# Remainders of projection weights kept in DRAM between the two halves of a sequence

## The chip, the cores and the metric

The kernel runs on one core of a Trainium2 chip. The metric is the device time of one execution in microseconds (us). Three runs of the kernel before took 1563.96, 1564.00 and 1564.34 us; the median is 1564.0 us.

The engines of the core are called here as the profile calls them: PE (TensorE, matrix products), DVE (VectorE), ACT (ScalarE), POOL (GpSimd) and SP (SyncE, which here only issues DMAs). Each engine runs its own instructions in order; a semaphore holds an instruction until what it needs has been done elsewhere, and everything behind it on that engine waits with it.

## What is computed

One layer of a decoder trunk, on 1024 rows of 1024 numbers in float32:

```
h = rms_norm(x, norm_mix)
proj = h @ w_in                        # 1024 x 8192
xa, ga, q, f, v, g, m_a, m_b = split(proj, 8 parts of 1024)
xa = causal_depthwise_conv(xa, conv_w, conv_b)
y_a = rg_lru(xa, w_r, b_r, w_i, b_i, lam) * gelu(ga)
o = rms_norm(hgrn2_chunkwise(silu(q), k(f), log_f(f), v), hg_norm)
y_b = o * silu(g)
y = sigmoid(m_a) * y_a + sigmoid(m_b) * y_b
x = x + y @ w_out
h = rms_norm(x, norm_mlp)
x = x + square(relu(h @ w_up)) @ w_down
out = rms_norm(x, norm_final)
```

`rg_lru` is a linear recurrence over the rows whose gates come from two block-diagonal products (`w_r`, `w_i`); `hgrn2_chunkwise` is gated linear attention with eight heads, done by blocks.

## The kernel before

**Products in two parts.** PE multiplies in a format with a shorter mantissa (`fp32r`). To keep float32's precision, each operand is split in a high part H, the value cast to `fp32r`, and a remainder L, the value less H. A product is then three matmuls, H by H, H by L and L by H (`mm3`, L131 to L136; in the profile the three lines are L134, L135 and L136). The split is made by `split` (L88 to L90): a cast on ACT (L89), then a subtraction on DVE (L90) that reads the raw value and the cast one.

**The mixer.** The first part of the program, up to about 520 us, makes the projections `xa`, `q`, `f`, `v` and the products of the recurrence's gates (`rg`), with the recurrence (`rg_lru`) and the attention (`hgrn`) beside them. The rows are in two chunks (`c`) of 512 and the heads in four pairs (`p`), so there are eight stages, chunk 0 with pairs 0 to 3 and then chunk 1 with pairs 0 to 3. Each pair has nine weight tiles of 128x1024 (512 KB): two each for `xa`, `q`, `f` and `v`, and one for `rg`. The list `pair_tiles` has the order of use; its 72 entries hold every one of the 36 tiles twice, once for each chunk, since the tiles aren't kept in between. The first half of the mixer is entries 0 to 35, the second half 36 to 71.

**Loading and splitting weights.** `load_w` takes one of four `raw` buffers and issues a load on SP's queue (L97). `split_w` takes two of six buffers (tag `w`) for H (`wH`) and L (`wL`) of the tile, and splits. `get_w` asks for a tile when PE's code comes to use it and has two more split ahead. A `raw` buffer is free when its cast and its subtraction are done; a `w` buffer is free when PE has done the last matmul that reads it. Which engine instruction comes where is set by a scheduler that simulates the program and takes priorities (`tc.high_priority`) and marks for program order (`tc.keep_in_program_order`) into account; PE's order in the mixer is pinned.

**Inside a stage.** `hgrn` of one pair runs while the next stage's projections run on PE: it is written as calls `go(n)` that let n steps of the next stage's generator pass, between blocks of its own products. The names that matter: `f`, `kk`, `q` are the gate, key and query tiles; `kc`, `qb`, `qf`, `seg` are products of them made on DVE (L508); `sc` are banks with the blocks' scores (L518, L637, L648); `pk` are the transposes of `kk` on PE (L674), copied by ACT to `kT` (L679); `pkv` are the key by value products (L684); `sn` are the states, and `po` the outputs. `kk` is scaled for the last time on DVE just before `pk`. The copy `kc` to `kk`, the convolution (`xc`, L413), the recurrence (`ri`, `rw`), and the subtractions for weight tiles share DVE with it. A stage begins with the `v` products of the pair before, which use the two `v` tiles together.

**SP's queue.** It holds, in one order, the loads of `raw`, of `x`, the stores of the recurrence's result (`hd`, L474), and the stores of sums and differences of the normed rows made on POOL for a later part (`cd`, L327).

Of the kernel before, what the change touches and what calls it, by code (L numbers as in the profile page):

```python
# [10 lines left out]
F32 = mybir.dt.float32  # L11
# [7 lines left out]
P = 128  # L19
# [27 lines left out]
def trunk(ctx: ExitStack, tc: tile.TileContext, x, wts, mlp, pv, gains, mask_f, mask_u, out):  # L47
    nc = tc.nc
    V, A, G, PE = nc.vector, nc.scalar, nc.gpsimd, nc.tensor
# [4 lines left out]
    dram = ctx.enter_context(tc.tile_pool(name="dram", bufs=1, space=DRAM))  # L54
# [12 lines left out]
    pair_tiles = []  # L67
    for i in range(NC * NPAIR):
        at = (0, 1, 2, 3, 4, 6, 5)
# [6 lines left out]
    for c in range(NC + 1):  # L76
        seq += [wts[MIX_TILES + j] for j in range(OUT_TILES)]
    most = [n_mix]
    ready, made = {}, [0]


    in_order = [True]
# [1 line left out]
    def keep(ins):  # L84
        if in_order[0]:
            tc.keep_in_program_order(ins)

    def split(src, h, lo):  # L88
        keep(A.copy(h, src))  # L89
        keep(V.tensor_tensor(out=lo, in0=src, in1=h.bitcast(F32), op=ALU.subtract))  # L90
# [9 lines left out]
    def split_w(i, raw):  # L100
        h = wp.tile([P, 1024], F32R, tag="w", name=f"wH{i}", bufs=6)
        lo = wp.tile([P, 1024], F32R, tag="w", name=f"wL{i}", bufs=6)
        with tc.high_priority(400):
            split(raw, h, lo)
        return h, lo

    raws = []

    def fill_w(n):
        while made[0] < min(n, most[0]):  # L110
            i = made[0]
            raw = raws.pop(0) if raws else load_w(i)
            ready[made[0]] = split_w(i, raw)
            made[0] += 1
# [650 lines left out]
    def stage(i):  # L765
        c, p = where(i)
        got = gots[i]
        if i == 0:
            yield from v_steps(c, p, got, lambda tt: None)
        elif i > 1:  # L770
            yield from v_of(i)

        def more(n):
            with tc.high_priority(400):
                transposed(xn1[n], hT[1], n, f"x1{n}")

        hooks = {at: lambda n=n: more(n) for at, n in {2: ((4, 1),), 3: ((2, 2), (6, 3))}.get(i, ())}
        px = yield from hooked(project_steps(c, f"xa{c}{p}"), hooks)
        xc, xps = conv_in(c, p, px)
        if i == 0:  # L780
            parameters()
            tc.keep_in_program_order(V.tensor_copy(mu, mu32.to_broadcast([P, 7, 8, 32])))
            pinned[0] = True
        yield
        if i == 1:
            gots[0]["tail"]()
            transposed(xn1[0], hT[1], 0, "x10")
        if i > 4:
            combos_on(2)

        def convolve():
            got["xc"] = conv(c, p, xc, xps, None)

        pq = yield from hooked(project_steps(c, f"q{c}{p}"), {} if i == 1 else {6: convolve})
        got["q1"] = q_of(c, p, pq)
        yield
        fs = hooked(project_steps(c, f"f{c}{p}"), {6: convolve} if i == 1 else {})
        for _ in range(5 if i != 1 else 7):
            next(fs)
            yield  # L800
        if i > 3:
            combos_on(1 if i == 4 else 2)
        if i == 1:
            pf = yield from fs
            got["f"], got["kk"] = f_of(c, p, pf)
            yield
        yield from rg_lru(c, p, got, *got["xc"])
        if i > 0:
            gots[i - 1]["normalised"]()
        for n in ((0,), (1,), (2, 3))[i] if i < 3 else ():  # L810
            xn1[n] = next_rows(n)
        if i != 1:
            pf = yield from fs
            got["f"], got["kk"] = f_of(c, p, pf)
# [14 lines left out]
    def last_stage():  # L829
        yield from v_of(NC * NPAIR)  # L830
        combos_on(2)
        w = [next_w(), next_w()]
        g2 = []
        for c in range(NC):
            pp = yield from plain(c, w, "g")
            g = mt(("xc", "h")[c], f"g2{c}", (P, 2, T))
            g2.append(g)
            for s in range(2):
                o = g[:, s if c == 0 else 1 - s, :]
                A.activation(o, pp[s], AF.Sigmoid)  # L840
                V.tensor_tensor(out=o, in0=o, in1=pp[s], op=ALU.mult)
            if c == 0:
                combos_on(1)
            yield
        w = [next_w(), next_w()]
        for c in range(NC):
            pp = yield from plain(c, w, "mb")
            g = g2[c]
            t = mt("ri", f"smb{c}", (P, 2, T))
            for s in range(2):  # L850
                A.activation(t[:, s if c == 0 else 1 - s, :], pp[s], AF.Sigmoid)
            V.tensor_tensor(out=g, in0=g, in1=t, op=ALU.mult)
            if c == 0:
                nc.scalar.dma_start(g2d[:, 0:2, :], g)
                gots[-1]["normalised"]()
                yield
        on_T(NC - 1, NPAIR - 1, gots[-1])
        nc.scalar.dma_start(g2d[:, 2:4, :], g2[1])
# [29 lines left out]
    for i in range(NC * NPAIR):  # L888
        rest = stage(i + 1) if i + 1 < NC * NPAIR else last_stage()
# [336 lines left out]
    rest = []  # L1226
# [320 lines left out]
```

## Time and profile before

| what | us |
|---|---|
| median of three runs | 1564.0 |
| the profiled execution | 1564.07 |
| its span, first to last instruction | 1562.2 |
| PE busy | 1523.0 |
| DVE busy | 1205.4 |
| ACT busy | 818.5 |
| POOL busy | 155.5 |

The span is the time from the first to the last instruction in the profile of one execution; the time of the same execution is 1.9 us longer. Busy times are sums over the span. PE's matmuls overlap, so a busy PE is not one at its peak. A row of a time line has its start, its length, engine and line, operation, tile written and tiles read, shape and count, and in brackets the idle time of the engine ahead of it with what ended it. Buffer numbers are left out of names in the profile, so `wL` there is any remainder tile of weights. Rows with SPq are issues of DMAs. A row of waits has who waited for whom, the sum in us, how often, and the longest. A row on a DMA issue has how often, the size, and the median time from issue to landing.

### The profile page before, as it was taken

Reading aid. Unit: us, or ns where it says so; the run is one execution under the profiler, and the core shown is the slowest. Engines: PE = TensorE matmul, PEld = TensorE weight load, DVE = VectorE, ACT = ScalarE, POOL = GpSimd, SP = SyncE. Lnnn points to the kernel's source line nnn. Section 1 sums busy time; section 2 is a strip of 40 time slices with the busy share of each in tenths; the row PEclk is TensorE's granted clock in tenths of the full one; section 3 lists DMA queues with packets and bytes.
Section 4 is the critical chain, followed back from the end, with each engine's and each line's share of the span. In section 5 each row is a group of like instructions: output and inputs, shape, how many; then the busy total and the mean of one; then the engine's idle time right before and its main releaser. Section 6 shows DMA issues by size and latency. Waiting matters only on the chain.

```text
span 1562.2 us, 23154 instructions
## 1 busy us (share of the span) xinstructions
PE 1523.0 (97%) x9072; PEld 1271.9 (81%) x9072; DVE 1205.4 (77%) x1706; ACT 818.5 (52%) x1341; POOL 155.5 (10%) x187
## 2 busy tenths in 40 slices
PE   7999999999999999999999989999999999999998
PEld 6878888888788887888888777888888878888886
DVE  5798596696786928786856589888888988888877
ACT  5657757557467435454533376777777631111113
POOL 1013110233624600000000000000000000000000
PEclk9999999999999999999999999999999999999999
DMA  6233233233442274432338862766666675666642
GB/s 235 97 105 109 68 109 108 79 122 120 141 136 95 95 289 181 137 135 81 135 108 308 283 216 99 298 252 250 245 243 242 226 286 225 252 253 253 252 192 108
DMA packets 75341, 280.07 MB, mean 179 GB/s; under 512 B 7776, under 2 KB 20192, under 8 KB 62304
## 3 DMA queue, kind: packets, MB, share of 16 engines
q1 hardware_dynamic: 72208, 267.58, 46.6%
q10 hardware_dynamic: 3024, 11.01, 1.9%
q8 instruction: 71, 1.16, 0.3%
q14 instruction: 38, 0.31, 0.1%
HBM read 193.63 MB, written 84.93 MB: 178 GB/s over the span
## 4 chain that ended last, share of the span: by engine, by line
PE 79%; DVE 11%; ACT 6%; issue 2%; DMA 2%; POOL 0%; DVEq 0%; SPq 0%; ACTq 0%; POOLq 0%
PE dX L134 4%; PE dX L135 4%; PE dX L136 4%; PE uX L134 3%; PE uX L135 3%; PE uX L136 3%; PE gX L134 3%; PE gX L135 3%; PE gX L136 3%; PE dY L135 2%; PE dY L136 2%; PE dY L134 2%; PE uY L134 2%; PE uY L135 2%; PE uY L136 2%
## 5 line engine op out<-in xcount | busy, mean ns | idle before, releaser
L90 DVE TENSOR_TENSOR wL<-raw,wH 128x1024 fp32r<-128x1024 f32 x100 | 123.9, 1240 | 76.2 <-ACT wH L89 75.8
L89 ACT CAST wH<-raw 128x1024 fp32r<-128x1024 f32 x100 | 104.9, 1049 | 78.7 <-PE po L135 26.2
L1456 DVE TENSOR_TENSOR acc<-acc,dX 128x512 f32<-128x512 f32 x128 | 85.1, 685 | 29.2 <-PE dX L136 28.9
L89 ACT CAST wA<-q 128x512 fp32r<-128x512 f32 x46 | 28.5, 621 | 139.1 <-PE dX L136 101.0
L1456 DVE TENSOR_TENSOR acc<-acc,dY 128x512 f32<-128x512 f32 x64 | 43.5, 686 | 15.7 <-PE dY L136 14.5
L136 PE MATMUL po<-wH,y 128*128 128x512 f32 x128 | 50.0, 391 | 0.0
L134 PE MATMUL po<-wH,y 128*128 128x512 f32 x128 | 50.0, 391 | 0.0
L135 PE MATMUL po<-wL,y 128*128 128x512 f32 x128 | 50.0, 391 | 0.0
L1321 ACT ACTIVATE b<-b 128x512 f32<-128x512 f32 x48 | 30.1, 630 | 29.5 <-DVE b L1320 29.4
L157 POOL TENSOR_TENSOR rstd_h<-rstd_h,mhalf 128x1 f32<-128x1 f32 x8 | 5.6, 700 | 379.0 <-DVE rstd_h L156 379.0
L90 DVE TENSOR_TENSOR wA<-q,wA 128x512 fp32r<-128x512 f32 x46 | 31.6, 687 | 13.6 <-ACT wA L89 13.6
L413 DVE SCALAR_TENSOR_TENSOR xc<-xp,pvt,xc 128x512 f32<-128x512 f32 x48 | 40.4, 862 | 0.0
L927 DVE TENSOR_TENSOR s<-q,q 128x512 f32<-128x512 f32 x46 | 31.6, 689 | 2.8 <-DMA q<-mlp_in 2.3
L326 POOL TENSOR_TENSOR stt<-r,stt 128x256 fp32r<-128x256 f32 x16 | 21.1, 1337 | 118.5 <-ACT stt L325 113.5
L932 DVE TENSOR_TENSOR s<-q 128x512 f32<-128x512 f32 x46 | 31.6, 688 | 0.3
L716 ACT ACTIVATE on<-po 128x128 f32<-128x128 f32 x64 | 16.9, 281 | 27.9 <-PE po L712 27.9
L1322 ACT ACTIVATE b<-b 128x512 f32<-128x512 f32 x48 | 30.0, 630 | 1.1
L136 PEld LDWEIGHTS po<-wH,y 128*128 128x128 f32 x128 | 24.1, 188 | 4.9
L135 PEld LDWEIGHTS po<-wL,y 128*128 128x128 f32 x128 | 24.0, 188 | 4.9
L134 PEld LDWEIGHTS po<-wH,y 128*128 128x128 f32 x128 | 24.0, 188 | 4.8
L615 ACT COPY kk<-kc 128x512 f32<-128x512 f32 x8 | 5.0, 622 | 43.1 <-DVE kc L508 43.1
L622 POOL TENSOR_SCALAR scT<-dd 32x256 f32<-32x256 f32 x32 | 21.5, 671 | 52.7 <-DVE dd L537 36.1
(2528 smaller groups left out, 5418.6 us busy)
## 6 DMA issues: line engine op xcount, KB each, us to landing
raw<-wts_in SPq DMA_DIRECT2D x96, 512.0 KB, 3.6
q<-mlp_in SPq DMA_DIRECT2D x92, 512.0 KB, 3.6
x<-x_in SPq DMA_DIRECT2D x8, 512.0 KB, 6.0
hd<-ri SPq DMA_DIRECT2D x16, 256.0 KB, 3.0
od<-onT ACTq DMA_DIRECT2D x8, 512.0 KB, 5.6
cdT<-stT SPq DMA_DIRECT2D x16, 256.0 KB, 3.6
o<-od SPq DMA_DIRECT2D x4, 1024.0 KB, 7.0
h<-hd SPq DMA_DIRECT2D x4, 1024.0 KB, 4.8
```

What stands on the lines that cost most here:

```text
L89: keep(A.copy(h, src))
L90: keep(V.tensor_tensor(out=lo, in0=src, in1=h.bitcast(F32), op=ALU.subtract))
L134: pin(PE.matmul(o, ah, bh, start=first, stop=False, **how))
L135: pin(PE.matmul(o, ah, bl, start=False, stop=False, **how))
L136: pin(PE.matmul(o, al, bh, start=False, stop=last, **how))
L413: ins = V.scalar_tensor_tensor(xc[:, s, :], xp[:, j : j + T], pvt[:, PV_CW + 8 * j + u : PV_CW + 8 * j + u + 1], xc[:, s, :], op0=ALU.mult ...
L622: G.tensor_scalar(scT[32 * b : 32 * b + 32, :, 32 * b : 32 * b + 32], dd[32 * b : 32 * b + 32, :, :], 1.0, 0.0, op0=ALU.mult, op1=ALU.add,)
L927: V.tensor_tensor(out=sa[:, 0, :], in0=a21, in1=a22, op=ALU.add)
L932: V.tensor_tensor(out=sb[:, 0, :], in0=a21, in1=a11, op=ALU.add)
L1321: A.activation(b[:, at, :], b[:, at, :], AF.Relu, scale=-1.0 if at == 2 else 1.0)
L1322: A.activation(b[:, at, :], b[:, at, :], AF.Square)
L1456: V.tensor_tensor(out=dst, in0=dst, in1=banks[bk, pr], op=op)
```

## The change

When a weight tile of the mixer is split for the first time, and the same tile comes again later in `pair_tiles`, its remainder is stored to a DRAM tile of its own. When it comes for the second time, only the cast is done; the remainder is loaded from DRAM into the L buffer. Both DMAs are issued on SP's queue. The numbers that the matmuls read are the same.

```
-    ready, made = {}, [0]
+    ready, made, rests = {}, [0], {}
...
     def split_w(i, raw):
         h = wp.tile([P, 1024], F32R, tag="w", name=f"wH{i}", bufs=6)
         lo = wp.tile([P, 1024], F32R, tag="w", name=f"wL{i}", bufs=6)
+        at = pair_tiles[i] if i < len(pair_tiles) else None
         with tc.high_priority(400):
+            if at in rests:
+                A.copy(h, raw)
+                nc.sync.dma_start(lo.bitcast(F32), rests[at])
+                return h, lo
             split(raw, h, lo)
+        if at is not None and at in pair_tiles[i + 1 :]:
+            rests[at] = dram.tile([P, 1024], F32, tag=f"rest{at}", name=f"rest{at}")
+            nc.sync.dma_start(rests[at], lo.bitcast(F32))
         return h, lo
```

In all, 36 subtractions leave DVE (100 of this form become 64), 36 stores join SP's queue in the first half, and 36 loads join it in the second half. A `raw` buffer of the second half is free when its cast is done. The lines of the kernel below the change move down by eight, so L508 becomes L516 and so on.

**DVE in the first stage of the second half that has the attention of chunk 1, pair 0.** The rows from the partial copies of scores (`dd`) to the last scaling of `kk`; the first number behind a name is its chunk and pair or its place in the list of tiles. Before:

```order
L537 COPY_PREDICATED dd10_3301<-mu_122,sc2_10_3611 128x32x2
L413 SCALAR_TENSOR_TENSOR xc11_3528<-xp13_3532,pvt_77,xc11_3528 128x512
L90 TENSOR_TENSOR wL50_3718<-raw50_3715,wH50_3717 128x1024
L537 COPY_PREDICATED dd10_3301<-mu_122,sc8_10_3644 128x8x24
L90 TENSOR_TENSOR xcL11_3742<-xc11_3528,xcH11_3741 128x1024
L537 COPY_PREDICATED dd10_3301<-mu_122,sc8_10_3644 128x8x16
L411 COPY xp14_4233<-xcar_124 128x3
L537 COPY_PREDICATED dd10_3301<-mu_122,sc8_10_3644 128x8x8
L487 SCALAR_TENSOR_TENSOR q111_3757<-sq11_3758,par_123,pj_q11_0_3591 128x256x2
L90 TENSOR_TENSOR wL51_3768<-raw51_3765,wH51_3767 128x1024
L487 SCALAR_TENSOR_TENSOR q111_3757<-sq11_3758,par_123,pj_q11_1_3592 128x256x2
L508 TENSOR_TENSOR kk10_3293<-kk10_3293,seg10_3303 128x8x64
```

DVE in the same place, now:

```order
L545 COPY_PREDICATED dd10_3373<-mu_122,sc2_10_3683 128x32x2
L90 TENSOR_TENSOR xcL11_3814<-xc11_3600,xcH11_3813 128x1024
L545 COPY_PREDICATED dd10_3373<-mu_122,sc8_10_3716 128x8x24
L419 COPY xp14_4305<-xcar_124 128x3
L545 COPY_PREDICATED dd10_3373<-mu_122,sc8_10_3716 128x8x16
L545 COPY_PREDICATED dd10_3373<-mu_122,sc8_10_3716 128x8x8
L495 SCALAR_TENSOR_TENSOR q111_3829<-sq11_3830,par_123,pj_q11_0_3663 128x256x2
L495 SCALAR_TENSOR_TENSOR q111_3829<-sq11_3830,par_123,pj_q11_1_3664 128x256x2
L516 TENSOR_TENSOR kk10_3365<-kk10_3365,seg10_3375 128x8x64
```

The subtractions of tiles 50 and 51 are gone, the last step of the convolution (`xc`) stands further up, and the rest is in nearly the same order.

**SP's queue in the second half, around the second `v` tile (tile 44) of the same stage.** `raw` with a number is the load of that tile. Before:

```order
L97 DMA raw46_3335<-wts_in 128x1024
L97 DMA raw47_3468<-wts_in 128x1024
L97 DMA raw48_3498<-wts_in 128x1024
L97 DMA raw49_3593<-wts_in 128x1024
L97 DMA raw50_3715<-wts_in 128x1024
L97 DMA raw51_3765<-wts_in 128x1024
```

SP's queue in the same place, now; `rest` with a number is the DRAM tile of that weight tile:

```order
L97 DMA raw46_3407<-wts_in 128x1024
L107 DMA wL43_3270<-rest7_157 128x1024
L97 DMA raw47_3540<-wts_in 128x1024
L107 DMA wL44_3291<-rest8_183 128x1024
L97 DMA raw48_3570<-wts_in 128x1024
L107 DMA wL45_3404<-rest9_600 128x1024
L97 DMA raw49_3665<-wts_in 128x1024
L107 DMA wL46_3410<-rest10_614 128x1024
L107 DMA wL47_3543<-rest11_730 128x1024
L97 DMA raw50_3787<-wts_in 128x1024
L97 DMA raw51_3837<-wts_in 128x1024
```

Each remainder's load has come into the row of `raw` loads, beside the `raw` load of a tile three or four places later.

**SP's queue at the start.** Loads of the rows (`x`), the parameters (`pvt`) and masks (`mf`, `mu32`) and the first weights. Before:

```order
L274 DMA x3_145<-x_in 128x1024
L211 DMA pvt_77<-pv_in 128x73
L212 DMA mf_121<-maskf_in 128x32
L215 DMA mu32_241<-masku_in 128x224
L97 DMA raw3_244<-wts_in 128x1024
L97 DMA raw4_356<-wts_in 128x1024
L300 DMA x4_638<-x_in 128x1024
L97 DMA raw5_386<-wts_in 128x1024
```

SP's queue in the same place, now:

```order
L282 DMA x3_145<-x_in 128x1024
L112 DMA rest7_157<-wL0_154 128x1024
L219 DMA pvt_77<-pv_in 128x73
L220 DMA mf_121<-maskf_in 128x32
L223 DMA mu32_247<-masku_in 128x224
L97 DMA raw3_250<-wts_in 128x1024
L97 DMA raw4_364<-wts_in 128x1024
L112 DMA rest8_183<-wL1_180 128x1024
L97 DMA raw5_396<-wts_in 128x1024
L308 DMA x4_660<-x_in 128x1024
```

The store of the first remainder stands ahead of the parameters, and the load of the fifth block of rows (`x4`, the first of the second half's rows) has moved behind the second store. On ACT and DVE the norms of `x4` and `x5` have moved back by a few rows accordingly; apart from that and the places shown, the order of ACT changes by a few casts by a place or two, POOL's not at all, and PE's by one matmul near the start.

## The prediction

> **What bounds the kernel now.** I read the page first, then TensorE's waits, then the time line around each wait, then the same stretches on VectorE, ScalarE and the load queue. The page's first lines:
>
> ```profile
> span 1562.2 us, 23154 instructions
> PE 1523.0 (97%) x9072; PEld 1271.9 (81%) x9072; DVE 1205.4 (77%) x1706; ACT 818.5 (52%) x1341; POOL 155.5 (10%) x187
> PEclk9999999999999999999999999999999999999999
> ```
>
> TensorE is busy in 97% of the span at the full granted clock, so a change to other engines gains only what TensorE waits for them, and at most there. The change touches the two halves of the mixer, up to about 520 us. In the second half, where work is removed, the view of waits for TensorE from 270 to 520 us has one row, and the time line says where its three waits are (the number in brackets is idle time ahead of the row):
>
> ```profile
> PE pk L674 <- DVE kk L508: 5.3, 3, 1.8
> ```
>
> ```profile
> 346.89 1.15 PE L648 MATMUL sc<-qf,kk 128*64 128x64 f32 x16
> ...
> 351.95 0.39 PE L136 MATMUL pj_f<-hT10H,wL 128*128 128x512 f32 x1
> 354.14 0.88 PE L674 MATMUL pk<-ident,kk 128*128 128x128 f32 x6 [1.79 <-DVE kk L508]
> ...
> 356.24 1.50 PE L684 MATMUL pkv<-v,kT 128*128 128x128 f32 x12
> ...
> 417.31 0.87 PE L674 MATMUL pk<-ident,kk 128*128 128x128 f32 x6 [1.71 <-DVE kk L508]
> ...
> 480.49 0.88 PE L674 MATMUL pk<-ident,kk 128*128 128x128 f32 x6 [1.78 <-DVE kk L508]
> ...
> 541.94 0.77 PE L674 MATMUL pk<-ident,kk 128*128 128x128 f32 x5
> ```
>
> TensorE comes to the transposes of `kk` three times before VectorE has scaled `kk`. The last stage, 480.49 to 541.94, ends with no such wait and lasts 61.45; the two ahead of it, from one `pk` to the next, last 63.17 and 63.18, longer by the wait. What VectorE does before the first of them:
>
> ```profile
> core 0: us, PE busy (x) PEld busy (x) DVE busy (x) ACT busy (x) POOL busy (x), PEclk, DMA share, GB/s
> 309.00:354.10 45.10, 43.23 (x453) 36.81 (x452) 43.17 (x67) 29.08 (x52) 15.97 (x16) 1.00 0.36 119
> ```
>
> ```profile
> 345.12 1.23 DVE L508 TENSOR_TENSOR qf<-qb,seg 128x512 f32<-128x512 f32 x1
> ...
> 347.41 1.75 DVE L90 TENSOR_TENSOR wL<-raw,wH 128x1024 fp32r<-128x1024 f32 x1
> ...
> 351.60 1.22 DVE L90 TENSOR_TENSOR wL<-raw,wH 128x1024 fp32r<-128x1024 f32 x1
> ...
> 353.40 0.68 DVE L508 TENSOR_TENSOR kk<-kk,seg 128x512 f32<-128x512 f32 x1
> ```
>
> VectorE is busy 43.17 of 45.10 us there: it is the bound of this chain, and the remainders of the weights (`wL`) stand inside it.
>
> **The change, part by part.** *36 subtractions go from the second half.* All subtractions of this form, and those in the stretch above alone (columns as above without ACT and POOL):
>
> ```profile
> L90 DVE TENSOR_TENSOR wL<-raw,wH 128x1024 fp32r<-128x1024 f32 x100 | 123.9, 1240 | 76.2 <-ACT wH L89 75.8
> ```
>
> ```profile
> 309.00:354.10 45.10, 23.48 (x68) 12.81 (x68) 8.88 (x7) 1.00 0.36 119
> ```
>
> 36 x 1.24 is 44.6 us of VectorE, but no gain by itself. On the path lie the seven of each stage, 8.88 us, ahead of a wait of 1.8. Two of them alone, at 347.41 and 351.60, are 2.97 us between `qf` and `kk`. What can still hold `kk`: the product at 346.89 reads it and ends at 348.04; the scaling of 0.68 would then end at 348.7, while TensorE, without its wait, comes to the transposes at 354.14 - 1.79 = 352.35. So the wait goes whole, with some 3.6 us to spare: 1.79 + 1.71 + 1.78 = 5.28 us gained. That is also the ceiling in this half, as there is no other wait in it.
>
> *What is late next* is the copy of the transposes (`kT`) on ScalarE, which `pkv` needs:
>
> ```profile
> 353.03 1.04 ACT L89 CAST wH<-raw 128x1024 fp32r<-128x1024 f32 x1
> 354.72 0.86 ACT L679 COPY kT<-pk 128x384 f32<-128x384 f32 x2 [0.65 <-PE pk L674]
> ```
>
> From `pk` to `pkv` TensorE takes 356.24 - 354.14 = 2.10 us, so it would be at `pkv` at 354.45. The cast ahead of `kT` needs the buffer that the matmul at 351.95 frees at 352.34; it then ends at 353.4 and the two copies at 354.3, in time. If the cast kept its old start of 353.03, the copies would end at 354.07 + 0.86 = 354.93, a wait of 0.48 in each of three stages, 1.4 us. I take nothing, since the sigmoids and copies ahead of the cast on ScalarE also move up with VectorE; nought and 1.4 are the ends.
>
> *36 loads come to the second half, on SP's queue.* A load waits until TensorE has freed the buffer, where the subtraction came behind a cast with the same wait. The shortest time from free buffer to use is at the second of the two `v` tiles, whose buffers the gate weights (`rg`) leave, four times (once in each of three stages, once in the last part):
>
> ```profile
> 366.40 0.39 PE L136 MATMUL pi<-xcH,wL 128*128 128x512 f32 x1
> ...
> 372.26 0.28 PE L135 MATMUL pv<-wL,hT11H 128*128 128x256 f32 x1
> ```
>
> Free at 366.79, used at 372.26: 5.47 us. Loads of the same size and shape, `raw`, from 300 to 500 us, and the longest kind of this size in the whole run:
>
> ```profile
> DMA to landing us min/median/max: 3.1/3.4/6.6
> ```
>
> ```profile
> y<-yd SPq DMA_DIRECT2D x8, 512.0 KB, 8.5
> ```
>
> At 3.4 us the load is there 2.1 us early, and costs nothing; the work that hides it is the rest of the `f` projection. If every one of the four took 6.6, TensorE would stop 4 x 1.13 = 4.5 us. I take nought, because the load is the first of a pair: the next `raw` is issued only when the cast, about 1 us long, has freed its buffer, and 6.6 is the landing of a second one. It can't gain either, as TensorE waits for no `wL` there. The ends are nought and 4.5. The Trainium skill, "DMA: Bandwidth & Descriptors", section "Latency and other measured facts", speaks against the change: it puts the access time of the memory at 0.2 us on average and 2 us at high load. Added in full to 3.4 that is an estimate of 5.2 us by that page, still inside 5.47, so the sum would stay, with a margin of 0.3 in place of 2.1; no run here shows it yet.
>
> *Queues.* On SP each such load now stands ahead of later `raw` loads and of the stores of `hd` and `cd`, and holds them until its buffer is free. SP's time line has the `raw` load due next at the place above:
>
> ```profile
> 368.98 4.50 SPq L97 DMA_DIRECT2D raw<-wts_in  x2
> ```
>
> Before, it was issued at 368.98, behind a subtraction; without that, it goes when the cast, 1.04 us in the row further up, has ended, about 367.8, just behind the remainder's load. No wait for a load appears on any engine between 250 and 520 us, so I cost the queue at nothing.
>
> *36 stores come to the first half.* Each waits on SP for the subtraction that makes it; the `raw` load behind it mostly waits for a subtraction too, of the same or an earlier tile. The one wait for a load from 27 to 250 us, one `raw` load on SP with its cast on ScalarE, and the nearest row for a store of this size:
>
> ```profile
> ACT xn L155 <- DMA x<-x_in: 0.4, 1, 0.4
> ```
>
> ```profile
> 26.65 0.33 SPq L97 DMA_DIRECT2D raw<-wts_in  x1
> ```
>
> ```profile
> 40.59 1.05 ACT L89 CAST wH<-raw 128x1024 fp32r<-128x1024 f32 x1
> ```
>
> ```profile
> yd<-yH SPq DMA_DIRECT2D x7, 512.0 KB, 3.5
> ```
>
> The wait is one of 0.4 us, and the `raw` tile issued at 26.65 is cast 14 us later, so a load held back by some microseconds is still early. The buffer of a remainder must now stay until its store has landed, 3.5 us; it is written again only after TensorE has used it up, later than that. Cost nought; above it, 1 us should the first stage shift.
>
> *The start.* What stands there on VectorE and TensorE:
>
> ```profile
> 9.35 1.22 DVE L90 TENSOR_TENSOR wL<-raw,wH 128x1024 fp32r<-128x1024 f32 x1
> ...
> 37.35 0.16 DVE L228 TENSOR_TENSOR par<-pvt 128x8 f32<-128x8 f32 x1
> ```
>
> ```profile
> 22.27 0.66 PE L164 MATMUL xT_x<-ident,xn 128*128 128x128 f32 x4 [0.21 <-DVE rstd_x L156]
> ```
>
> The first store stands ahead of the loads of the parameters, and holds them until the first subtraction is done, at 10.57; their first reader is at 37.35, 27 us later. Two norms of the second half's rows move back behind work of the first stage; of the 0.21 us that TensorE waits there, part may go. Between -0.2 and +1 us; I take nought. **Sum:** -5.3. The profiled execution took 1564.07 us, 1.9 around its span of 1562.2; the median of the runs is 1564.0, the same. The span would be 1556.9 and the time 1558.8.
>
> **The rivals.** *The loads come late (slower).* Place: the second `v` tile, four times. Price: four times what landing exceeds 5.47. From 6.8 us on it eats the 5.3; from 7.6 (4 x 2.13 = 8.5, less 5.3) the kernel is slower by 0.2%. At 8.5, as the eight `y` loads that are queued together, it is 4 x 3.03 = 12.1, less 5.3: 1570.8. For it: the bytes in flight double in places. Against: `raw` loads land in 3.4, and DMA is busy 0.36 of the time.
>
> *Some come late.* Landing at 6.6, the longest of the `raw` loads: 4.5 less 5.3, 1563.3, not to be told from before. The page named above would bring this only if its 2 us came on top of a second load in flight.
>
> *The wait moves to `pkv`.* 1.4 of 5.3 comes back: 1560.2. For it: the cast stands ahead of `kT` on ScalarE. Against: its buffer is free 0.7 us before its old start.
>
> *The change doesn't reach the path.* Were `kk` held by something other than VectorE's queue, the three waits would stay: 1564.0. Against: 96% busy, and `kk` follows a subtraction within 1.8 us.
>
> **How the numbers follow.** Forecast 0.71; `pkv` 0.06; some loads late 0.07; no reach 0.05; loads late 0.11. A measurement of this kernel tells 0.2%, 3.1 us, from no change, so faster means below 1560.9: 0.71 + 0.06 = 0.77; within 0.07 + 0.05 = 0.12; slower 0.11. The time is the likeliest case's, 1558.8. The range goes down by 1 us, for the start's 0.2 and small waits that I can't see, and up to 1563.3, which takes in the second and third case and leaves 0.16 out.
>
> **What would show it.** Right: no wait of `pk` for `kk` in the second half, stages of 61.4 us there, 64 subtractions of the form above instead of 100, loads of `wL` that land in under 5.4 us, no TensorE wait for one, and the first half's rows where they were. Wrong: idle time at `pv<-wL` or `pkv`, a cast that waits for `raw`, or a first `pk` later than before.

## The result, and the profile after

The changed kernel takes 1562.5 us (median of 20 runs), the kernel before 1565.0 (median of 20): a ratio of 0.9983, 95% interval 0.9977 to 0.9990. That is 1.6 to 3.6 us faster, about half of the 5.3 us forecast. The time lies within the range given, 3.7 us above the predicted one. The gain of 0.17% falls short of the 0.2% from which the prediction speaks of faster, a case to which it gave 0.77; what came is the case "within", to which it gave 0.12.

The first lines of the page of the changed kernel, and its row for the subtractions (lines stand 8 further down than before):

```profile
span 1560.8 us, 23272 instructions
PE 1521.7 (97%) x9072; PEld 1271.4 (81%) x9072; DVE 1167.3 (75%) x1670; ACT 819.0 (52%) x1341; POOL 148.8 (10%) x187
L90 DVE TENSOR_TENSOR wL<-raw,wH 128x1024 fp32r<-128x1024 f32 x64 | 78.3, 1223 | 50.7 <-ACT wH L89 47.9
```

The row for the subtractions has 36 fewer and 45.6 us less, where the prediction had 44.6. VectorE as a whole is busy only 38.1 us less, so its other instructions became some 7.5 us longer in sum. The view of TensorE's waits from 120 to 500 us has one row, and it is a new one; the time line of TensorE shows both of its stops, and the three places where `pk` waited for `kk` before:

```profile
PE sc L526 <- issue: 2.2, 2, 1.3
```

```profile
149.66 0.76 PE L526 MATMUL sc<-qb,kc 128*32 128x48 f32 x51
151.27 0.37 PE L526 MATMUL sc<-qb,kc 128*32 128x48 f32 x13 [0.85 <-issue]
...
275.43 0.78 PE L526 MATMUL sc<-qb,kc 128*32 128x48 f32 x52
277.56 0.36 PE L526 MATMUL sc<-qb,kc 128*32 128x48 f32 x12 [1.35 <-issue]
...
355.02 0.28 PE L682 MATMUL pk<-ident,kk 128*128 128x128 f32 x1
...
416.24 0.39 PE L682 MATMUL pk<-ident,kk 128*128 128x128 f32 x2
...
477.56 0.39 PE L682 MATMUL pk<-ident,kk 128*128 128x128 f32 x2
```

The three waits are gone. In their place TensorE stops twice in the middle of a run of 64 short matmuls, after the 51st and after the 52nd, and waits for nothing that a semaphore explains ("issue"). The kernel before ran both of these runs through: at 149.65 all 64 are one group of 0.86 us, and the matmul behind it starts at 150.44. In the changed kernel that matmul starts at 151.57, 1.12 us later from the start of the run, so the stop costs some 0.3 us more than its idle time of 0.85.

Since the end of the mixer varies from one execution to the next (below), I read the loss and the gain off at the third of these `pk`, the last that waited. It starts at 480.49 before and at 477.56 after: 2.93 us earlier. By stages, from one `pk` to the next: the one that holds the first stop became longer by 59.06 - 57.95 = 1.11, the one with the second by 63.08 - 61.42 = 1.66, and the three without a wait shorter by 5.7 together. 5.7 - 2.8 = 2.9.

### The profile page after: what moved, and what is told of

Its sections match the earlier page's. It is cut to its first block, busy times and chain, and to the rows that moved or that the text cites. A ratio compares the mean times of both kernels' runs of the same rounds, so it can differ in the third digit from the quotient of the medians.

```text
span 1560.8 us, 23272 instructions
## 1 busy us (share of the span) xinstructions
PE 1521.7 (97%) x9072; PEld 1271.4 (81%) x9072; DVE 1167.3 (75%) x1670; ACT 819.0 (52%) x1341; POOL 148.8 (10%) x187
## 4 chain that ended last, share of the span: by engine, by line
PE 81%; DVE 9%; ACT 6%; issue 2%; DMA 1%; POOL 0%; DVEq 0%; POOLq 0%; ACTq 0%; SPq 0%
PE dX L142 4%; PE dX L143 4%; PE dX L144 4%; PE uX L142 3%; PE uX L143 3%; PE uX L144 3%; PE gX L142 3%; PE gX L143 3%; PE gX L144 3%; PE pj_q L142 2%; PE dY L143 2%; PE dY L142 2%; PE dY L144 2%; PE pj_q L143 2%; PE pj_xa L143 2%
## 5 line engine op out<-in xcount | busy, mean ns | idle before, releaser
L90 DVE TENSOR_TENSOR wL<-raw,wH 128x1024 fp32r<-128x1024 f32 x64 | 78.3, 1223 | 50.7 <-ACT wH L89 47.9
L334 POOL TENSOR_TENSOR stt<-r,stt 128x256 fp32r<-128x256 f32 x16 | 14.7, 942 | 124.6 <-ACT stt L333 111.9
L1022 DVE TENSOR_TENSOR gb<-gY,ge 128x512 f32<-128x512 f32 x14 | 9.7, 690 | 21.8 <-PE gY L144 21.1
```

## The experiments

Two theories stood at the start. A: the gain on the path is whole, and the added transfers hold up the blocks of TensorE's own instructions, which come by DMA too. B: the loss follows from VectorE running earlier, above all in the last stage, where some of its instructions were stretched. C was kept as a third: the stops are chance.

**e1: the stores alone.**

```diff
         with tc.high_priority(400):
-            if at in rests:
-                A.copy(h, raw)
-                nc.sync.dma_start(lo.bitcast(F32), rests[at])
-                return h, lo
             split(raw, h, lo)
```

> The 36 stores of the first half stay; the second half makes its remainders by subtraction again, so the three waits of pk for kk (5.3 us) stay. Theory A (the change gains its 5.3 us, and the added transfers give about 2.7 of it back, by short stops of TensorE that no semaphore explains, 0.85 us at 151 and 1.35 us at 277 us): the first stop comes with the stores, so this kernel is slower than before by about 1 us (0.5 to 1.5), with a stop near 151 us and none near 277. Rival B (the stores and loads cost nothing; what is given back comes from VectorE's earlier work in the last stage, which then meets GpSimd): the same time as before within 0.3 us. Rival C (the stops come and go from one execution to the next and belong to no part): the same as before, with stops at other places or none.

Measured: 1565.3 us, ratio 1.0005 (0.9996 to 1.0014). TensorE's waits from 120 to 500 us:

```profile
PE pk L678 <- DVE kk L512: 5.3, 3, 1.8
PE sc L522 <- issue: 0.9, 1, 0.9
```

The stop at 151.27 is there, the one near 277 is not, and the third `pk` starts 1.09 us later than before. The time alone doesn't tell 0.7 us from none; the trace does. VectorE's work is that of before, so the stop comes with the stores.

**e2: the loads, with one store.** All 36 loads read the first remainder.

```diff
-        if at is not None and at in pair_tiles[i + 1 :]:
-            rests[at] = dram.tile([P, 1024], F32, tag=f"rest{at}", name=f"rest{at}")
-            nc.sync.dma_start(rests[at], lo.bitcast(F32))
+        if at is not None:
+            if not rests:
+                rests[at] = dram.tile([P, 1024], F32, tag=f"rest{at}", name=f"rest{at}")
+                nc.sync.dma_start(rests[at], lo.bitcast(F32))
+            rests[at] = rests[pair_tiles[0]]
```

> One remainder alone is stored, and the second half loads that one 36 times in the place of each of its own (so all remainders there but one are wrong values); VectorE does no subtraction there. It is the change without 35 of its 36 stores. Theory A (loads and stores each give something back): faster than before by 3.5 to 4 us, about 1 us faster than the whole change, with a stop near 277 us and none near 151. Rival B (nothing is given back by transfers, but by VectorE's new place in the last stage): faster by 2.5 to 3 us, just as the whole change. Rival C (the stops belong to no part): faster by 4 to 5.3 us, and the whole change too when it is taken again.

Measured: 1560.7 us, ratio 0.9975 (0.9966 to 0.9985), 3.9 us faster. The stop at 151 is gone. There are two in the half with the loads, one of them where the whole change has none, and a third of 0.2 us at 400.79, in the `q` projection; the first two:

```profile
275.49 0.36 PE L528 MATMUL sc<-qb,kc 128*32 128x48 f32 x12 [0.54 <-issue]
...
461.19 0.71 PE L528 MATMUL sc<-qb,kc 128*32 128x48 f32 x45 [1.50 <-issue]
```

Stores and loads each bring stops of their own, and their sum, 0.7 slower and 3.9 faster, each with about 1.4 us either way, is about the whole change. A has this right; the stops at 461 and 400 it had not foreseen.

**e3: neither store nor load,** the remainder left out in the second half, with the rounded weight in its place.

```diff
-        lo = wp.tile([P, 1024], F32R, tag="w", name=f"wL{i}", bufs=6)
         at = pair_tiles[i] if i < len(pair_tiles) else None
+        lo = None if at in rests else wp.tile([P, 1024], F32R, tag="w", name=f"wL{i}", bufs=6)
         with tc.high_priority(400):
             if at in rests:
                 A.copy(h, raw)
-                nc.sync.dma_start(lo.bitcast(F32), rests[at])
-                return h, lo
+                return h, h
             split(raw, h, lo)
-        if at is not None and at in pair_tiles[i + 1 :]:
-            rests[at] = dram.tile([P, 1024], F32, tag=f"rest{at}", name=f"rest{at}")
-            nc.sync.dma_start(rests[at], lo.bitcast(F32))
+        if at is not None:
+            rests[at] = True
         return h, lo
```

> No store and no load is added; the second half casts the weights and multiplies with the rounded weight in the place of the remainder, so the remainder is left out of the computation there. The same matmuls run. It is the ceiling of the change. Theory A: the whole 5.3 us, 4.8 to 5.5 faster than before, and no stop in the last stage. Rival B (what is given back comes from VectorE running earlier in the last stage, where its instructions are stretched by about 0.5 us each beside GpSimd): 2.5 to 3.5 faster, as the change itself, with the waits of 1.3 and 0.8 us near 524 and 541 us still there.

Measured: 1564.2 us, ratio 1.0000 (0.9991 to 1.0009). No theory had that. It isn't the ceiling that I meant it to be: without the buffer of the remainder the order on ScalarE and the look-ahead on the weights change, and TensorE has other waits (240 to 500 us):

```profile
PE sc L654 <- ACT qf L622: 2.8, 3, 1.7
PE pv L140 <- ACT kk L505: 2.0, 4, 1.1
PE pk L680 <- DVE kk L514: 1.9, 3, 0.7
```

ScalarE's time line ahead of the first of them shows why: the copies of `kk` and `qf` stand behind casts of `stt` that wait for GpSimd.

```profile
346.81 0.41 ACT L331 CAST stt<-r 128x256 fp32r<-128x256 f32 x1 [1.88 <-POOL r L323]
347.13 0.61 ACT L621 COPY kk<-kc 128x512 f32<-128x512 f32 x1
347.65 0.40 ACT L331 CAST stT<-r 128x256 fp32r<-128x256 f32 x1
347.96 0.61 ACT L622 COPY qf<-qb 128x512 f32<-128x512 f32 x1
```

So e3 speaks neither for B nor against it. It has no stop of the "issue" kind, and no transfers; that much agrees with A.

**e4: six remainders.** Only those whose subtraction stands between the two scalings of `kk`.

```diff
-        if at is not None and at in pair_tiles[i + 1 :]:
+        if at is not None and at in [pair_tiles[j] for j in (50, 51, 59, 60, 68, 69) if j > i]:
```

> Only the six remainders whose subtraction stands between the two scalings of kk in the three stages that wait (tiles 50, 51, 59, 60, 68 and 69 of the order) are stored and loaded; the other 30 of the second half are subtracted as before. 6 MB of traffic in place of 36. All theories: VectorE has 2.97 us less between qf and kk, so the three waits of 1.8 go. Theory A (traffic gives back the rest): 4.8 to 5.3 us faster than before, 2 us faster than the whole change. Rival B (the last stage gives it back, which follows here its old order with its subtractions): 5.3 us faster too, but without it in e3. Rival C (nothing belongs to a part): 4 to 5.3 faster, as the whole change taken again.

Measured: 1562.9 us, ratio 0.9991 (0.9982 to 1.0000). No stop, but each of the three waits is only halved:

```profile
PE pk L682 <- DVE kk L516: 2.9, 3, 1.0
```

All theories were wrong on this, and my prediction would have been too: it named only the product at 346.89 as what can still hold `kk`. On VectorE's time line `kk` now follows a `q` that waits for a sigmoid, and on ScalarE the two sigmoids stand behind the cast of `xc`:

```profile
352.10 0.75 DVE L495 SCALAR_TENSOR_TENSOR q<-sq,par,pj_q 128x512 f32<-128x512 f32 x1 [0.69 <-ACT sq L493]
352.77 0.68 DVE L516 TENSOR_TENSOR kk<-kk,seg 128x512 f32<-128x512 f32 x1
```

```profile
347.68 1.05 ACT L89 CAST xcH<-xc 128x1024 fp32r<-128x1024 f32 x1 [1.79 <-DVE xc L421]
348.75 1.28 ACT L493 ACT_TABLE_LOAD   x1
350.04 0.60 ACT L493 ACTIVATE sq<-pj_q 128x512 f32<-128x512 f32 x1
350.53 1.04 ACT L106 CAST wH<-raw 128x1024 fp32r<-128x1024 f32 x1
351.47 0.60 ACT L493 ACTIVATE sq<-pj_q 128x512 f32<-128x512 f32 x1
```

In the whole change that cast stands ahead of the copies of `kk` and `qf`, 5.7 us earlier (341.96), because VectorE reaches `xc` earlier. The wait needs both: the subtractions gone, and VectorE early enough for that order.

**e5 and e9: nine remainders,** a third one in each stage, run twice. The edit is against the whole change, as in e4.

```diff
-        if at is not None and at in pair_tiles[i + 1 :]:
+        if at in [pair_tiles[j] for j in (49, 50, 51, 58, 59, 60, 67, 68, 69) if j > i]:
```

> Nine remainders in place of 36 are stored and loaded: tiles 49 to 51, 58 to 60 and 67 to 69 of the order, three in each stage that waited. With six (e4) a wait of 0.95 us was left in each stage, because on ScalarE the cast xcH stood between the copy of qf and the two sigmoids whose products VectorE makes ahead of kk; with the third tile of each stage gone from VectorE, the cast stands ahead of qf, as in the whole change. Theory A (the change frees 5.3 us, and TensorE loses 2.2 us again where its instruction fetches queue behind the added transfers, at 151 and 277 us): no wait of pk for kk, no stop at 151 or 277, and 4.8 to 5.3 us faster than before. Rival B (the loss lies in VectorE's order in the last stage, or in every kernel that frees VectorE): no faster than the whole change, 2.5 us. Rival C (the loss comes from one execution to the next): as the whole change taken again.

> The nine remainders of e5 again, for a tighter ratio, since e5 had five undisturbed runs. Theory A (5.3 to 5.8 us gained on the path, nothing lost to stops): 0.9960 to 0.9967. If e5 was a lucky draw: 0.9975 to 0.9983, as the whole change.

Measured: 1558.2 us, ratio 0.9964 (0.9951 to 0.9976), and again 1557.3 us, ratio 0.9952 (0.9939 to 0.9964). No wait and no stop on TensorE from 120 to 500 us in either profile, and the third `pk` at 474.69 and 474.86, 5.8 and 5.6 us earlier than before. This version beats both kernels, by 5.6 and 7.5 us in the middle of its two ratios, with a quarter of the transfers. Theory A holds; the second ratio lies beyond its 0.9960 to 0.9967, which the interval reaches into.

**e6: the whole change without four of its remainders,** those whose transfers stand just ahead of the two stops.

```diff
-        if at is not None and at in pair_tiles[i + 1 :]:
+        if at in [pair_tiles[j] for j in range(36, 72) if j > i and j not in (39, 40, 56, 57)]:
```

> The whole change, but the four remainders whose transfers stand just ahead of the two stops are subtracted as before: tiles 39 and 40 (loaded at 266 and 271 us) and 56 and 57 (their first-half remainders were stored at 138 and 141 us). None of the four stands between qf and kk in a stage that waits. Theory A (instruction fetches queue behind transfers): the stops at 151 and 277 go or shrink below 0.3 us, the fetches start earlier there, and the kernel is 4 to 5.3 us faster than before. Rival B: the stops belong to the code at these places and stay, 2.5 us faster as the whole change. Rival C: stops at other places in each execution.

Measured: 1559.4 us, ratio 0.9971 (0.9958 to 0.9983), 4.5 us faster. Both stops are gone, with 32 of the 36 remainders still going both ways, and the third `pk` starts at 474.82, as early as with nine. What differs is how full the DMA engines are ahead of the first stop. The stretch from 141 to 149 us, the columns being its length, busy time of TensorE, its weight loads, VectorE, ScalarE and GpSimd, the granted clock, the DMA share and GB/s; before, after, and e6:

```profile
141.00:149.00 8.00, 8.00 (x99) 6.18 (x101) 5.50 (x11) 4.15 (x7) 3.83 (x6) 1.00 0.67 211
```

```profile
141.00:149.00 8.00, 8.00 (x99) 6.17 (x100) 5.50 (x11) 4.17 (x7) 3.83 (x6) 1.00 1.00 345
```

```profile
141.00:149.00 8.00, 8.00 (x103) 6.19 (x105) 5.50 (x10) 4.12 (x7) 3.82 (x6) 1.00 0.71 261
```

At 0.67 and 0.71 TensorE runs on; at 1.00 it stops soon after. The same from 262 to 276 us, ahead of the second: 0.60 before, 0.96 after, 0.70 in e6. A full stretch alone does not bring a stop: from 450 to 460 us the share is 0.96 in e6 and in e7, ahead of the run of short matmuls at which e2 stops, and both run through. What stands in the full queues can be named: the page has a DMA queue that carries instructions.

```profile
q8 instruction: 71, 1.16, 0.3%
```

Its 71 packets of 16 KB are TensorE's: with 9072 matmuls and 9072 weight loads they come to 256 instructions each. The places of the stops bear this out. Among TensorE's records, 2241 stand ahead of the matmul with which it goes on after the stop near 151 us, in each of the four profiles that have it; 4545 stand ahead of the one near 277, and 7873 ahead of e2's near 461. The differences, 2304 and 3328, are 9 and 13 times 256. The record of packets gives the start and length of the one that each stop waits for:

```
                     fetch starts   took   ends     TensorE goes on   later by
before                  146.94      1.25   148.19   (no stop)
before, again (e8)      147.47      1.05   148.52   (no stop)
e5, nine                147.16      0.96   148.12   (no stop)
e6, without four        147.33      0.94   148.27   (no stop)
after                   148.90      0.93   149.83   151.27            1.44
after, again (e7)       148.50      0.88   149.38   150.99            1.61
e1, stores              148.86      0.95   149.81   151.27            1.46
e10, stores twice       151.19      0.93   152.12   153.61            1.49
after, second stop      275.12      0.92   276.04   277.56            1.52
after, again, second    274.59      0.94   275.53   276.89            1.36
e2, first stop          273.04      0.93   273.97   275.49            1.52
e2, second stop         458.77      0.95   459.72   461.19            1.47
```

In all eight cases TensorE goes on 1.4 to 1.6 us after the end of such a packet (at e2's small stop too: 399.29 and 400.79), and in the kernels without a stop at 151 the packet starts 1 to 2 us earlier than in the two profiles of after. To take out how far each kernel has got, the start can be counted from TensorE's own place, 256 records ahead of the matmul at which a stop would stand. Near 151 us the packet then starts 1.0 to 1.6 us later in the eight profiles without a stop, and 2.4 to 4.0 us later in the four with one. Near 277 and 461 us it is 0.6 to 1.8 without a stop and 2.4 to 3.6 with one, over all twelve profiles. The Trainium skill, "Runtime: NRT & Kernel Launch", section "Instruction fetch mechanics", says that each engine fetches its instructions in blocks of 16 KiB through a DMA queue of its own while it executes, and that the cost of a block is mostly hidden. The trace agrees on block and queue; here the cost is hidden only as long as the other queues leave the DMA engines room.

**e7 and e8: after and before once more.**

> The changed kernel once more, beside the others on one chip. Theory A: the stops at 151.3 and 277.6 us stand at the same places with about the same sizes (0.85 and 1.35 us), and the gain is 2 to 3.3 us. Rival C: other places, or none. The last stage (63.85 us in the first profile, 61.45 before) tells whether its extra 2.4 us belong to the change or to one execution: if they belong to it, 63.5 to 64.2 again; if not, it may be 61.4 to 64.

> The kernel before once more, for a second profile. The three waits of pk for kk at 354, 417 and 480 us again, 1.7 to 1.8 each, and no stop of TensorE without a releaser. If the last stage's length belongs to one execution, it may be anything from 61.4 to 64 us here; if it belongs to the kernel, 61.4 to 61.5 again.

Measured: after 1561.9 us, ratio 0.9982 (0.9972 to 0.9991); before 1564.4 in one run. TensorE's waits from 120 to 500 us, after and before:

```profile
PE sc L526 <- issue: 1.3, 2, 1.0
```

```profile
PE pk L674 <- DVE kk L508: 5.2, 3, 1.7
```

The two stops are at the same two places, of 0.34 and 1.00 us this time, and `pk` starts 3.56 us earlier than in e8. So C is wrong on the places; the sizes vary, which A had not said. And the last stage, 61.45 us in the first profile of before, is 63.91 in the second one, with the same waits of 1.3 us at `sc` and 0.8 at `pk` in it as in the profile after; the kernel with nine remainders shows both lengths as well, 63.84 in e5 and 61.44 in e9. So the extra 2.4 us come without the change too, and differ between executions of one kernel. That was what B rested on. Whether the change makes them more frequent is not shown.

**e10: each remainder stored twice,** with the second half of e1.

```diff
             nc.sync.dma_start(rests[at], lo.bitcast(F32))
+            again = dram.tile([P, 1024], F32, tag=f"again{at}", name=f"again{at}")
+            nc.sync.dma_start(again, lo.bitcast(F32))
```

> As e1 (the remainders are stored in the first half, and the second half subtracts them again), but each remainder is stored twice, to two places: 72 stores in place of 36, VectorE's work unchanged. Theory A (instruction fetches of TensorE queue behind the transfers): the first stop, 0.87 us at 151 in e1, grows to 1.2 us or more, and others may appear at short matmuls (sc<-qb,kc) near 92, 212 and 275 us; slower than before by 1.5 to 4 us, against 0.7 in e1. Rival B (the stops are a matter of the code's place): as e1, 1565.3 us, one stop of 0.9 us. If the stores begin to hold the raw loads as well, casts wait for raw and the loss is above 4 us.

Measured: 1571.3 us, ratio 1.0037 (1.0026 to 1.0048), 5.8 us slower, more than theory A gave; the profiled execution, at 1567.5, is the fastest of its eight. The stop has doubled, it is the only one, and no cast waits for `raw`:

```profile
PE pk L680 <- DVE kk L514: 5.2, 3, 1.8
PE sc L524 <- issue: 1.9, 1, 1.9
PE poT L392 <- ACT on L737: 0.4, 1, 0.4
```

The stage is longer by 4.96, though. The stretches behind the stop show another part of it (columns as above):

```profile
152.00:154.00 2.00, 0.39 (x14) 0.32 (x14) 1.10 (x3) 0.00 (x0) 0.00 (x0) 1.00 1.01 395
154.00:156.00 2.00, 2.00 (x6) 1.57 (x7) 1.97 (x4) 0.62 (x1) 0.00 (x0) 0.61 1.04 422
156.00:158.00 2.00, 2.00 (x7) 1.55 (x6) 1.99 (x4) 0.62 (x1) 0.00 (x0) 0.54 0.97 393
```

Behind the stop TensorE was granted half its clock for 3.4 us, which costs another 1.7: 1.88 + 1.7 + 0.4 is 4.0 of the 4.96, and the rest is open. After the shorter stops the clock stayed at 1.00.

## Why the prediction was right, and where not

*The gain on the path was right.* The three waits went whole, and nothing took their place at `pk` or `pkv`. Forecast 5.28 us; measured 5.6 to 5.8 at the third `pk` in the kernels without stops (e5, e6, e9), since each stage also became up to 0.25 us shorter than its wait explains. I have not looked into that.

*How the wait goes was right only in part.* The prediction looked at the product that reads `kk` and took the rest of VectorE's queue as free to move up. e4 shows a second holder: `q`, by way of the sigmoids on ScalarE. That it did no harm rests on the cast of `xc` having moved too. The 3.6 us to spare were not there either: at the first of the three places `kk` was done 2.7 us ahead of `pk` in the profile after, where TensorE had been held up by its stops, and 1.3 us ahead in e5.

*The loads themselves were as forecast.* Nothing waits for one. The loads of remainders from 250 to 500 us:

```profile
DMA to landing us min/median/max: 3.2/4.2/5.8
```

The median is 0.8 above the 3.4 taken, the longest within the ends given, though 3 of the 35 took more than the 5.4 us that the prediction names as a sign of being right. At the second `v` tile, with the 5.47 us of room, they landed 1.1 to 2.2 us ahead of use: the tightest was issued at 490.20, took 4.3, and is read at 495.64. The estimate that the prediction works out from the Trainium skill ("DMA: Bandwidth & Descriptors", section "Latency and other measured facts"), 5.2 us (3.4 with 2 us in the place of 0.2), lies between the median and the longest.

*The step that failed* is the one on the stores, "Cost nought; above it, 1 us should the first stage shift", together with "I cost the queue at nothing" for the loads. Both asked only who waits for the transfers themselves, by semaphores. The runs show 1.1 us lost in the first half with the stores (after, e1) and 1.7 in the second with the loads (0.9 and 1.3 in the second profile, e7), because TensorE's own instructions come through the same DMA engines. The trace of before had what was needed to ask: the instruction queue on its page, the runs of 64 short matmuls, and a DMA share of 0.6 to 0.7 just ahead of two of them, to which the change adds half a megabyte every few microseconds. The forecast compared the load with a mean share of 0.36 from another stretch. One of the prediction's signs of being wrong did come, by way of this step: the first of the three `pk` starts later than before, at 355.02 in place of 354.14.

*The rivals:* none of the four named this. Their times of 1560.2 and 1563.3 lie on both sides of the result, but neither of their mechanisms occurred. That the range holds the result is luck: its upper end was set by loads that come late, and nothing waited for one.

## What to carry to other kernels

TensorE's instructions are transfers too: before traffic is added, look at the DMA share just ahead of each run of many short matmuls. The stops came behind stretches with a share of 0.87 to 1.01, and none came behind those of up to 0.77 at the same three places. Move only what stands on the path: nine tiles gave the whole gain, and 36 gave half of it away. And when work is taken out of a queue, ask for the next holder on every engine that feeds it, since the order elsewhere may decide.

## What the runs showed of the hardware

- *Instruction blocks queue behind data.* With a DMA share of 0.87 to 1.01 in the 8 to 14 us ahead, the block for TensorE started 2.4 to 4.0 us behind the place from which it is counted above, in place of 0.6 to 1.8, and TensorE stopped for 0.3 to 1.9 us, in seven of eight cases after the 51st or 52nd of 64 short matmuls. At 0.96 it did not always: e6 and e7 ran through near 461 us, the block 1.6 and 1.5 us behind.
- *A stop can cost the clock.* After 1.88 us with little work the granted clock was 0.5 for 3.41 us; after stops of up to 1.5 it was not. The kernel before shows the same stretch of 3.41 us at 938 us, behind a wait of 2.39 us; the changed kernel has that wait, of 2.38, and no such stretch. All twelve profiles have the wait and four the stretch, so the length of the stop alone doesn't decide it.
- *A slow load goes with a longer stage.* The last stage took 60.9 to 61.5 us in five profiles and 63.5 to 63.9 in seven, the kernel before among both. In the first profile of before, a load of 512 KB (`q<-mlp_in`) landed in 3.6 us, in the second in 5.2, with one packet of 4 KB in it that took 1.9 us where the median is 0.16. VectorE then waits for it, and its instructions are stretched from there on, while two of GpSimd's beside them (`stt`) take 3.36 us in the second profile and 7.89 in the first. VectorE's time line, first profile of before and e8:

```profile
515.61 0.70 DVE L927 TENSOR_TENSOR s<-q,q 128x512 f32<-128x512 f32 x1
516.21 0.43 DVE L508 TENSOR_TENSOR qb<-qa,seg 128x256 f32<-128x256 f32 x1
```

```profile
516.49 0.98 DVE L927 TENSOR_TENSOR s<-q,q 128x512 f32<-128x512 f32 x1 [0.87 <-DMA q<-mlp_in]
517.39 0.96 DVE L508 TENSOR_TENSOR qb<-qa,seg 128x256 f32<-128x256 f32 x1
```

The same product takes 0.43 us in the one and 0.96 in the other. In all seven profiles with the long stage this load took 4.4 us or more, in four of the five others 3.4 to 3.8; in e3 it comes at another place. In the second profile of after (e7) it took 4.4 with no packet above 0.9. Why the load is slow is open, and that the load is the cause was not tried by moving it.
